# Moving the activations of the projections to another place in SBUF, by gaps between the pools

## The chip, the cores and the metric

The kernel runs on one core of a Trainium2 chip. The metric is the device time of one execution in microseconds. Three executions of the kernel before took 1711.0, 1717.55 and 1719.35 us, a median of 1717.55. A fourth one was taken by the hardware profiler: it took 1714.88 us, of which the profile's span covers 1713.1.

## The reference, cut to what matters

Three transformer blocks follow each other on one sequence of 256 tokens with 1024 features, all in float32:

```python
x = first_block(x, ...)    # forgetting attention, then sparse attention with compressed keys
x = second_block(x, ...)   # stick-breaking and dilated attention, then a gated feed-forward layer
return third_block(x, ...) # pooling and attention branches, then peer_ffn

def peer_ffn(h, w_q, sub_keys, u_tab, v_tab):
    q = (hf @ w_q).reshape(T, PEER_HEADS, 2, PEER_HALF)
    ...                    # two top-16 lists per head, their 16 best sums, softmax: e_c, g_c
    a = gelu(einsum('cd,chkd->chk', x_c, u_tab[e_c]))
    return einsum('chk,chkd->cd', g_c * a, v_tab[e_c])
```

The kernel does not gather the experts of `peer_ffn`: it multiplies the tokens with all 16,384 rows of `u_tab` and of `v_tab` and weights the experts that were not chosen with zero. So nearly all of its work is matrix products of 256 tokens with float32 weights that are read once from HBM.

## The kernel before, in words

**Weights.** The weights come in a fixed list of blocks of 128x1024 float32 (512 KB). `Weights.split` (lines 228 to 245) loads a block into `wraw` and splits it: ScalarE rounds it to fp32r, a format of TensorE with fewer bits, into `whi` (line 241), and VectorE writes the rest to `wlo` (line 242). Each split block has a number, counted from 0. `whi` and `wlo` lie in the pool `part`, which has three places for each; a block whose number leaves 3 when divided by 4 lies in the pool `extra` instead, as long as the number is under `until`, which comes to 232 (line 238). Block numbers 248 to 375 are those of `u_tab`, 376 to 503 those of `v_tab`.

**Products.** An activation is split in the same way into `hxh` and `hxl`, each 128 partitions x 8 x 256. A product of two split numbers is three matmuls, with the weights as the stationary operand (128x128) and the activation as the moving one (256 columns): `mm3`, lines 448 to 452. A weight block in `proj` is 8 times `mm3`, 24 matmuls. In the feed-forward layer `down` (lines 1204 to 1206) does the same with `fah` and `fal` as the moving operand. In `proj_nat` (lines 496 to 498) and in the last stage (line 1624) the roles are swapped: the activation is stationary and the weights move, 512 columns at a time.

**Stages in order of time.** Up to some 870 us the program has the five layers ahead of `peer_ffn`: projections whose results feed an attention that is woven between the matmuls, or the feed-forward layer (about 510 to 695 us). From some 874 us follow the queries of `peer_ffn` (16 blocks); then `proj(128, hx, ...)` (line 1601) multiplies with `u_tab`, and between its matmuls, every 42 of them or so, stand 12 matmuls of 128 columns (line 1584) that spread the gate weights over the experts. From 1355 us on, line 1624 multiplies with `v_tab`.

**Where tiles lie.** Pools lie behind each other in SBUF in the order in which they are opened; a tile's address is the same in all 128 partitions. Two pools hold split activations: `hxp` (line 279, the outer one, with inputs of projections) and `hxe` (line 1693, outputs of attention that enter the out-projections and the tile `mg`). `wp` (line 1605), the activations of the last stage, takes the place of `hxl` in `hxp`. The tiles of a layer (`ph`, with `fah` and `fal` among them) are allotted behind `extra`. The order of the program's instructions on an engine is the order in which the Python code issues them.

Of the kernel before, what the change touches and what calls it, by code (L numbers as in the profile page):

```python
# [9 lines left out]
F32 = mybir.dt.float32  # L10
F32R = mybir.dt.float32r
# [7 lines left out]
P = 128  # L19
D = 1024  # L20
S = 256
# [184 lines left out]
class Weights:  # L206
# [40 lines left out]
    def next(self):  # L247
        self.split(self.nu + 1 + self.ahead)
        self.nu += 1
        return self.p.pop(self.nu - 1)  # L250
# [20 lines left out]
def program(tc, A, out, upto=99):  # L271
    nc = tc.nc
    ctx = ExitStack()
    with ctx:
        cst = ctx.enter_context(tc.tile_pool(name="cst", bufs=1))
        big = ctx.enter_context(tc.tile_pool(name="big", bufs=1))
        raw = ctx.enter_context(tc.tile_pool(name="raw", bufs=4))
        part = ctx.enter_context(tc.tile_pool(name="part", bufs=3))
        hxp = ctx.enter_context(tc.tile_pool(name="hxp", bufs=1))
        ps = ctx.enter_context(tc.tile_pool(name="ps", bufs=2, space=PSUM))  # L280

# [1095 lines left out]
        def peer(hx, ph, hp):  # L1377
# [224 lines left out]

            tc.keep_in_program_order(nc.scalar.preload_act_table_set("natural_log_exp_and_others"))
            xN, gf = token_major()
            wp = hxp.tile([P, 3, 2, S], F32R, name="hxl")
            acc = [[ps.tile([P, 512], F32, name=n) for _ in range(2)] for n in ("s", "t")]
            chunks = {}

# [30 lines left out]
        def token_major():  # L1639

            xN = hxp.tile([P, 2, D], F32, name="hxh")
            for tb in range(2):
                for h in range(2):
                    p = ps.tile([P, 512], F32, name="o")
                    for k in range(4):
                        nc.tensor.transpose(p[:, k * P:k * P + P], xT[:, 4 * h + k, tb * P:tb * P + P], ident)
                    nc.scalar.copy(xN[:, tb, h * 512:h * 512 + 512], p)
            gf = [xT[:, 4 * i:4 * i + 4, :].rearrange("p a b -> p (a b)") for i in range(2)]
            for h in range(2):
                p = ps.tile([P, 512], F32, name="pj")  # L1650
                for k in range(4):
                    nc.tensor.matmul(p[:, k * P:k * P + P], mod(5)[:, 4 * h + k:4 * h + k + 1].to_broadcast([P, P]), ident,
                                     start=True, stop=True)
                nc.scalar.copy(gf[0][:, h * 512:h * 512 + 512], p)
            nc.sync.dma_start(gf[1], A["fin3"].to_broadcast([P, D]))
            return xN, gf
# [33 lines left out]
        with ExitStack() as early:  # L1690
            cp = early.enter_context(tc.tile_pool(name="cp", bufs=1))
            wk = early.enter_context(tc.tile_pool(name="wk", bufs=3))
            hxe = early.enter_context(tc.tile_pool(name="hxe", bufs=1))
            W.extra = early.enter_context(tc.tile_pool(name="extra", bufs=1))
            con = cp.tile([P, A["consts"].shape[1]], F32, name="con")
            nc.sync.dma_start(con, A["consts"])
            off = 0
            for n, m in CONSTS.items():
                C[n] = con[:, off:off + m]
                off += m  # L1700
            st = Rms(V["g0"])
            for kt in range(8):
                st.parts(kt)
                if kt == 0:
                    W.split(1)
            for i, blk in enumerate((fox, nsa, mixer2, ffn2, mixer3)):
                if i >= upto:
                    break
                i_blk = i
                if i == 2:  # L1710
                    cbp = tc.alloc_tile_pool(name="cbp", bufs=1)
                with tc.tile_pool(name=f"ph{i}", bufs=1, reuse_waits="tile") as ph:
                    st = blk(st)
                if i == 3:
                    cbp.release()
        if upto > 5:
            with tc.tile_pool(name="ph5", bufs=1, reuse_waits="tile") as ph, tc.tile_pool(name="hp", bufs=1, reuse_waits="tile") as hp:
                st = peer(st, ph, hp)
            with tc.tile_pool(name="ph6", bufs=3, reuse_waits="tile") as ph:
                wk = ph  # L1720
                finish_peer(*st)
        else:
            nc.sync.dma_start(out, xT)
# [5 lines left out]
def build(ins, upto=99):  # L1729
    import concourse.bacc as bacc  # L1730
    nc = bacc.Bacc("TRN2", target_bir_lowering=False, num_devices=1)
    A = {k: nc.dram_tensor("in_" + k, v.shape, mybir.dt.from_np(v.dtype), kind="ExternalInput").ap()
         for k, v in ins.items()}
    out = nc.dram_tensor("out_0_dram", (P, 2, D) if upto > 5 else (P, 8, S), F32, kind="ExternalOutput").ap()
    with tile.TileContext(nc) as tc:
        program(tc, A, out, upto)
    return nc
# [9 lines left out]
```

## Time and profile before

| | |
|---|---|
| median of three executions | 1717.55 us |
| profiled execution, its span | 1714.88 us, 1713.1 us |
| TensorE (PE) matmuls busy | 1658.1 us, 97% of the span |
| VectorE (DVE) busy | 1304.1 us, 76% |
| ScalarE (ACT) busy | 976.3 us, 57% |
| mean load of DMA | 175 GB/s |

How to read the rows below. A row of part 5 of the page or of a list of waits says what it holds in words: line, engine, operation, tiles; then the busy time of all, the mean of one, and the idle time just ahead of them with its cause. A row of the timeline gives a start in us, a length in us, and the instruction; x12 means twelve of them merged in one row. Matmuls are pipelined: the next one starts while the one before is still under way, so the pace of TensorE is the distance between two starts, not the length. A row of the table of stretches gives the stretch, its length, the busy time of PE, PEld (weight loads), DVE, ACT and POOL with the number of instructions, the granted clock of TensorE (1.00 is full), the share of DMA and its GB/s.

### The profile page before, as it was taken

What the parts mean: (1) busy time and instruction counts of PE and PEld (TensorE: products, weight loads), DVE (VectorE), ACT (ScalarE), POOL (GpSimd) and SP (SyncE); (2) the same over time, 40 slices, a digit from 0 to 9 for tenths busy, and PEclk for the clock granted to TensorE, in tenths of its full rate; (3) what the DMA queues carried; (4) which work ended last, traced back from release to release, by engine and by line L of the source; (5) the groups of instructions that cost most, each with busy time, mean ns of one, the idle gap of its engine ahead of it and who ended that gap; (6) DMA issues with size and microseconds to landing.
All of it is one profiled execution on the core that took longest, in us unless ns stands there. A gap on an engine that the chain in (4) does not pass through costs nothing.

```text
span 1713.1 us, 31723 instructions
## 1 busy us (share of the span) xinstructions
PE 1658.1 (97%) x12052; PEld 1532.3 (89%) x12052; DVE 1304.1 (76%) x2715; ACT 976.3 (57%) x1853; POOL 189.4 (11%) x198
## 2 busy tenths in 40 slices
PE   9999999989899999999999999999999999999997
PEld 7999888778789999889999999999999988888886
DVE  6887878699867766786768988888999566666665
ACT  5775567558855555566544455554444555555554
POOL 2000244340130000111046000000000000000000
PEclk9999999999999999999999999999999999999999
DMA  7444542387437877435555555454454556555663
GB/s 252 136 136 150 169 166 64 105 268 243 149 111 259 267 262 245 143 118 173 175 172 161 161 164 157 159 161 156 155 161 159 174 195 196 190 193 195 196 189 120
DMA packets 84088, 300.07 MB, mean 175 GB/s; under 512 B 10144, under 2 KB 11040, under 8 KB 83680
## 3 DMA queue, kind: packets, MB, share of 16 engines
q1 hardware_dynamic: 83360, 296.39, 53.5%
q8 instruction: 94, 1.54, 0.4%
q10 hardware_dynamic: 576, 1.66, 0.3%
q14 instruction: 58, 0.48, 0.1%
HBM read 296.04 MB, written 1.05 MB: 173 GB/s over the span
## 4 chain that ended last, share of the span: by engine, by line
PE 52%; DVE 3%; ACT 0%; issue 0%; POOLq 0%; POOL 0%; DVEq 0%; ACTq 0%
PE s L1624 10%; PE t L1624 10%; PE pj L450 5%; PE pj L451 5%; PE pj L452 5%; PE o L1584 3%; PE s L450 2%; PE t L450 2%; PE s L452 2%; PE s L451 2%; PE t L451 2%; PE t L452 2%; DVE wlo L242 1%; PE s L1433 0%; PE o L595 0%
## 5 line engine op out<-in xcount | busy, mean ns | idle before, releaser
L241 ACT CAST whi<-wraw 128x1024 fp32r<-128x1024 f32 x504 | 528.9, 1051 | 359.0 <-PE pj L451 108.7
L242 DVE TENSOR_TENSOR wlo<-wraw,whi 128x1024 fp32r<-128x1024 f32 x486 | 601.1, 1241 | 168.2 <-ACT whi L241 165.7
L450 PE MATMUL pj<-hxh,whi 128*128 128x256 f32 x1448 | 417.0, 288 | 7.0 <-DVE vl L602 4.5
L452 PE MATMUL pj<-hxh,wlo 128*128 128x256 f32 x1448 | 410.5, 284 | 1.2 <-DVE wlo L242 0.9
L451 PE MATMUL pj<-hxl,whi 128*128 128x256 f32 x1448 | 410.8, 284 | 0.6 <-DVE hxl L1193 0.3
L450 PEld LDWEIGHTS pj<-hxh,whi 128*128 128x128 f32 x1448 | 276.4, 191 | 11.6 <-DVE vl L602 5.4
L451 PEld LDWEIGHTS pj<-hxl,whi 128*128 128x128 f32 x1448 | 276.2, 191 | 2.7 <-DVE hxl L1193 1.0
L452 PEld LDWEIGHTS pj<-hxh,wlo 128*128 128x128 f32 x1448 | 276.0, 191 | 2.9 <-DVE wlo L242 1.7
L1624 PE MATMUL s<-whi,hxl 128*128 128x512 f32 x512 | 157.8, 389 | 0.0
L1624 PE MATMUL t<-whi,hxl 128*128 128x512 f32 x512 | 157.6, 389 | 0.0
L1612 ACT CAST hxl<-a 128x256 fp32r<-128x256 f32 x128 | 52.1, 408 | 152.0 <-PE t L1624 150.2
L450 PE MATMUL s<-hxh,whi 128*128 128x256 f32 x456 | 130.7, 287 | 1.7 <-DVE st L572 1.7
L452 PE MATMUL s<-hxh,wlo 128*128 128x256 f32 x456 | 129.0, 283 | 0.4 <-DVE wlo L242 0.4
L451 PE MATMUL s<-hxl,whi 128*128 128x256 f32 x456 | 128.9, 283 | 0.0
L450 PE MATMUL t<-hxh,whi 128*128 128x256 f32 x432 | 124.6, 288 | 1.3 <-ACT whi L241 1.3
L452 PE MATMUL t<-hxh,wlo 128*128 128x256 f32 x432 | 122.8, 284 | 1.7 <-DVE wlo L242 1.5
L451 PE MATMUL t<-hxl,whi 128*128 128x256 f32 x432 | 122.4, 283 | 0.0
L1624 PEld LDWEIGHTS t<-whi,hxl 128*128 128x128 f32 x512 | 96.1, 188 | 19.9
L1624 PEld LDWEIGHTS s<-whi,hxl 128*128 128x128 f32 x512 | 95.9, 188 | 20.0 <-ACT hxl L1612 0.2
L1613 DVE TENSOR_TENSOR hxl<-a,hxl 128x256 fp32r<-128x256 f32 x128 | 54.3, 425 | 62.6 <-PE t L1624 60.5
L291 DVE SCALAR_TENSOR_TENSOR wraw<-wraw,cb 128x1024 f32<-128x1024 f32 x48 | 59.6, 1241 | 44.5 <-DMA wraw<-in_ada 44.2
L450 PEld LDWEIGHTS s<-hxh,whi 128*128 128x128 f32 x456 | 87.0, 191 | 2.1 <-issue 1.9
(409 smaller groups left out, 3401.5 us busy)
## 6 DMA issues: line engine op xcount, KB each, us to landing
wraw<-in_pu SPq DMA_DIRECT2D x128, 512.0 KB
wraw<-in_pv SPq DMA_DIRECT2D x128, 512.0 KB
wraw<-in_b_ffn SPq DMA_DIRECT2D x66, 512.0 KB
wraw<-in_ada SPq DMA_DIRECT2D x48, 512.0 KB
wraw<-in_b_qk SPq DMA_DIRECT2D x24, 512.0 KB
wraw<-in_fox_qk SPq DMA_DIRECT2D x16, 512.0 KB
wraw<-in_b_o SPq DMA_DIRECT2D x16, 512.0 KB
wraw<-in_b_g SPq DMA_DIRECT2D x16, 512.0 KB
```

What stands on the lines that cost most here:

```text
L241: nc.scalar.copy(hi, r)
L242: (nc.gpsimd if self.np in self.on_pool else nc.vector).tensor_tensor(lo, r, hi.bitcast(F32), op=OP.subtract)
L291: nc.vector.scalar_tensor_tensor(t, t, 1.0, cb, op0=OP.mult, op1=OP.mult, accum_out=modT[:, i:i + 1])
L450: nc.tensor.matmul(o, wh, xh, start=start, stop=False)
L451: nc.tensor.matmul(o, wh, xl, start=False, stop=False)
L452: nc.tensor.matmul(o, wl, xh, start=False, stop=stop)
L1584: nc.tensor.matmul(p[:, t, :], x[:, w[0], :, w[1]], y[i][:, w[0], :, w[1]], start=i == 0 and t == 0, stop=i == 2, skip_group_check=True)
L1612: nc.scalar.copy(ah, src)
L1613: nc.vector.tensor_tensor(al, src, ah.bitcast(F32), op=OP.subtract)
L1624: nc.tensor.matmul(acc[tb][h], x[:, t], w[:, h * 512:h * 512 + 512], start=n == 0 and i == 0, stop=n == P - 1 and i == 2)
```

## The change

The change adds five unused tiles ("gaps") between pools and shifts `wp` inside its tile by 16 elements (64 bytes). No instruction is added, removed or moved on any engine, and the waits of all instructions are the same; what differs is the SBUF addresses.

```diff
         part = ctx.enter_context(tc.tile_pool(name="part", bufs=3))
+        gaps = iter(range(9))
+
+        def gap(ctx, n):
+            ctx.enter_context(tc.tile_pool(name=f"gap{next(gaps)}", bufs=1)).tile([P, n // 4], F32, name="gap")
+
+        gap(ctx, 192)
         hxp = ctx.enter_context(tc.tile_pool(name="hxp", bufs=1))
...
-            wp = hxp.tile([P, 3, 2, S], F32R, name="hxl")
+            wp = hxp.tile([P, 16 + 6 * S], F32R, name="hxl")[:, 16:].rearrange("p (n i s) -> p n i s", n=3, i=2)
...
             wk = early.enter_context(tc.tile_pool(name="wk", bufs=3))
+            gap(early, 192)
             hxe = early.enter_context(tc.tile_pool(name="hxe", bufs=1))
+            gap(early, 64)
             W.extra = early.enter_context(tc.tile_pool(name="extra", bufs=1))
+            gap(early, 192)
```

The addresses that the pools give in the two programs, in bytes within a partition, and what is left of them modulo 256:

| tiles | before | after |
|---|---|---|
| `whi`, `wlo` in `part` | 43,296 and steps of 4,096: 32 | the same: 32 |
| `whi`, `wlo` in `extra` | 132,960 and 137,056: 96 | 133,408 and 137,504: 32 |
| `hxh`, `hxl` in `hxp` | 67,872 and 76,064: 32 | 68,064 and 76,256: 224 |
| `hxh`, `hxl` in `hxe` | 116,576 and 124,768: 96 | 116,960 and 125,152: 224 |
| `fah`, `fal` of the feed-forward layer | 152,416 and on, steps of 1,024: 96 | 153,056 and on: 224 |
| `wp` | 76,064 and steps of 1,024: 32 | 76,320 and on: 32 |

The parts of a tile that one matmul reads start at multiples of 512 or 1,024 bytes in it, so they have the same remainder. The distance from the weights to the activation, modulo 256, of the program's matmuls:

| matmuls | activation and weights in | before | after |
|---|---|---|---|
| 6,168 of `mm3` | `hxp` with `part` or `hxe` with `extra` (32 less 32, 96 less 96) | 0 | 192 |
| 720 of `mm3` | `hxe` or a layer's tiles with `part` | 64 | 192 |
| 840 of `mm3` | `hxp` with `extra` | 192 | 192 |
| 408 and 120 of `down` | `fah`, `fal` with `part` and with `extra` | 64 and 0 | 192 |
| 1,536 of line 1624 | `wp` with `part` | 0 | 0 |

The 288 matmuls of `proj_nat`, in which the weights move, have the distance from activation to weights at 0 (216 of them) or 64 (72, block in `extra`) before, and all at 64 after.

## Rows read from the trace of the kernel before

**Rows 1.** The page: busy time by engine, and two groups of matmuls.

```profile
PE 1658.1 (97%) x12052; PEld 1532.3 (89%) x12052; DVE 1304.1 (76%) x2715; ACT 976.3 (57%) x1853; POOL 189.4 (11%) x198
...
L450 PE MATMUL pj<-hxh,whi 128*128 128x256 f32 x1448 | 417.0, 288 | 7.0 <-DVE vl L602 4.5
...
L1624 PE MATMUL s<-whi,hxl 128*128 128x512 f32 x512 | 157.8, 389 | 0.0
```

**Rows 2.** What PE waited for, longest first: the first two.

```profile
PE pj L450 <- DVE vl L602: 4.5, 2, 3.4
PE t L616 <- POOL pn L578: 3.2, 3, 1.4
```

**Rows 3.** Stretches: attention, feed-forward, routing, `u_tab` early and late.

```profile
300.00:420.00 120.00, 110.89 (x745) 95.84 (x744) 100.10 (x212) 75.83 (x162) 35.74 (x42) 0.99 0.62 207
520.00:700.00 180.00, 176.56 (x1464) 174.89 (x1463) 127.39 (x185) 94.99 (x143) 0.00 (x0) 1.00 0.77 253
960.00:1000.00 40.00, 36.95 (x301) 35.16 (x300) 39.71 (x72) 19.77 (x32) 0.00 (x0) 1.00 0.56 173
1000.00:1040.00 40.00, 40.00 (x382) 39.70 (x380) 31.17 (x70) 21.58 (x50) 0.00 (x0) 1.00 0.48 158
1200.00:1320.00 120.00, 120.00 (x1131) 119.05 (x1130) 114.11 (x231) 56.02 (x131) 0.00 (x0) 1.00 0.49 159
```

**Rows 4.** Timeline of PE in the `u_tab` stage, one round.

```profile
1005.59 0.86 PE L1584 MATMUL o<-ohy,ohx 128*128 128x128 bf16 x12
1006.26 0.36 PE L450 MATMUL t<-hxh,whi 128*128 128x256 f32 x1
1006.46 0.28 PE L451 MATMUL t<-hxl,whi 128*128 128x256 f32 x1
...
1007.40 0.28 PE L450 MATMUL pj<-hxh,whi 128*128 128x256 f32 x1
...
1010.64 0.86 PE L1584 MATMUL o<-ohy,ohx 128*128 128x128 bf16 x12
```

**Rows 5.** Timeline of PE, feed-forward layer: blocks 135 and 136.

```profile
553.31 0.28 PE L450 MATMUL pj<-hxh,whi 128*128 128x256 f32 x1
...
556.04 0.28 PE L450 MATMUL pj<-hxh,whi 128*128 128x256 f32 x1
...
558.92 0.28 PE L1204 MATMUL s<-fah,whi 128*128 128x256 f32 x1
```

**Rows 6.** Timeline of PE, feed-forward layer: block 127, behind block 126.

```profile
530.46 0.28 PE L450 MATMUL o<-hxh,whi 128*128 128x256 f32 x1
...
533.28 0.28 PE L1204 MATMUL s<-fah,whi 128*128 128x256 f32 x1
```

**Rows 7.** Timeline of PE, third block: two stretches of three blocks in `part`.

```profile
825.02 0.28 PE L450 MATMUL pj<-pph,whi 128*128 128x256 f32 x1
...
833.50 0.28 PE L450 MATMUL pj<-pph,whi 128*128 128x256 f32 x1
...
858.45 0.28 PE L450 MATMUL pj<-hxh,whi 128*128 128x256 f32 x1
...
866.61 0.28 PE L450 MATMUL t<-hxh,whi 128*128 128x256 f32 x1
```

**Rows 8.** Timeline of PE, first attention: block 15 behind three transposes.

```profile
58.84 0.49 PE L616 MATMUL t<-ident,pn 128*128 128x128 f32 x3
59.08 0.37 PE L450 MATMUL pj<-hxh,whi 128*128 128x256 f32 x1
...
59.52 0.28 PE L450 MATMUL pj<-hxh,whi 128*128 128x256 f32 x1
...
60.55 0.39 PE L628 MATMUL o<-pth,vh 128*128 128x512 f32 x1
```

**Rows 9.** Timeline of PE, `proj_nat`: end of block 2, all of block 3.

```profile
18.10 0.39 PE L496 MATMUL s<-whi,hxh 128*128 128x512 f32 x1
...
18.78 0.40 PE L496 MATMUL s<-whi,hxh 128*128 128x512 f32 x1
...
21.54 0.40 PE L496 MATMUL s<-whi,hxh 128*128 128x512 f32 x1
```

## The prediction

> **What bounds the kernel now.** I read the page first: PE is busy for 1658.1 of 1713.1 us, and its largest groups are the 256-column matmuls of `mm3` and the 512-column ones of line 1624 [rows 1]. Then the list of what PE waited for: the longest entry is 4.5 us in total, the next 3.2 [rows 2]. So PE waits for almost nobody by name; it is bound by its own pace. The table of stretches says where another engine is close: in the `u_tab` stage PE is busy for 40.00 of 40 us while DVE has 31.17, but DVE reaches 39.71 of 40 in the routing stretch and 114.11 of 120 late in the stage [rows 3]. In the attention stretches PE itself has holes (110.89 of 120). The granted clock is 1.00 or 0.99 in all of them, the 2.4 GHz level, so the clock is no part of the argument. Last I read the timeline for the distance between starts, since that is what PE's pace is.
>
> **What the pace depends on in the trace.** The kernel before already contains every distance between activation and weights of the table, except the ones beyond 256 bytes, so the trace can be asked.
>
> At distance 0 (the `u_tab` stage), 27 matmuls (nine times `mm3`) lie between 1007.40 and 1010.64 us: 3.24 us / 27 = 120.0 ns each [rows 4]. Block 136, in `part`, does the same in another layer: 558.92 - 556.04 = 2.88 us / 24 = 120.0 ns [rows 5].
>
> At distance 192 (block 135, in `extra`, right ahead of it, same activation): 556.04 - 553.31 = 2.73 us / 24 = 113.8 ns [rows 5]. But block 127, also at 192, takes 533.28 - 530.46 = 2.82 us / 24 = 117.5 ns [rows 6].
>
> At distance 64 there are the same two paces, and each holds over a long stretch: 72 matmuls in 8.48 us, 117.8 ns, and 72 in 8.16 us, 113.3 ns [rows 7].
>
> So I read it thus: at 0 the pace is 120.0 ns and nothing else; at 64 and 192 it is one of two, 113.3 (quick) or 117.8 (slow), and a stretch keeps what it began with until something breaks the run. What chooses? Block 127 is slow and comes directly behind a block at distance 0, without a break; block 135 is quick and starts behind other matmuls. Block 15, also at 192, starts afresh behind three transposes, and is at (60.55 - 59.52) / 9 = 114 ns after a few matmuls [rows 8]. After the change no block at distance 0 is left to inherit from, and in the `u_tab` stage every round starts afresh: the first matmul behind the 12 of line 1584 lasts 0.20 us to the next start (1006.26 to 1006.46), as the one behind the transposes does (59.08 to 59.29) [rows 4, 8]. I take the quick pace there. Elsewhere I take the middle, 115.6 ns, since both occur.
>
> One rule speaks against all this. The Trainium skill, page SBUF — State Buffer, section "Who interferes with whom", says that PE has two independent read ports, one for the moving operand and one for weight loads, and that "PE and ACT never wait on anyone". By that rule addresses don't matter and the time would stay at 1714.9 us. Rows 5 show two blocks of the same instructions, the same activation and no wait, 2.73 and 2.88 us long, so the trace disagrees.
>
> **The change part by part**, against the profiled execution's 1714.9 us:
>
> 1. `u_tab` stage and queries: (16 + 128) blocks x 24 = 3,456 matmuls go from distance 0 to 192. at the quick pace, 113.6 ns as the mean of 113.8 and 113.3, 120.0 - 113.6 = 6.4 ns each: -22.1 us. Part of it is not to be had, since DVE's work doesn't shrink. From 960 to 1000 us DVE is idle for 0.3 us, so nearly all of that stretch's saving is lost (some 250 of the 301 matmuls are of 256 columns, 250 x 6.4 ns = 1.6 us; +1.3). From 1200 to 1320 us it is idle for 5.9 us, and PE would save about 840 x 6.4 ns = 5.4 us: PE would ask for nearly all of DVE's idle time, of which I expect two thirds to be usable (+2). What is late then is the one-hot products that line 1584 reads. Net -18.8.
> 2. The other 6,168 - 3,456 = 2,712 matmuls at 0, ahead of 870 us: 120.0 - 115.6 = 4.4 ns, -11.9 us. In the attention stretches PE is in a hole for some 8% of the time, and a faster PE meets its softmax partners earlier and waits for them; I take off a quarter: -9.
> 3. The 720 of `mm3` and 408 of `down` at 64 go to 192: two paces before, two after, 0. If all were quick before and slow after, 1,128 x 4.5 ns = +5; the reverse -5. The 120 of `down` at 0: -0.5.
> 4. `proj_nat`: 216 matmuls of 512 columns go from 0 to 64. At 0 three take 18.78 - 18.10 = 0.68 us, 227 ns each; at 64 the twelve of block 3 take 2.76 us, 230 ns [rows 9]. 216 x 3 = +0.65.
> 5. Line 1624: `wp` is shifted so that its remainder stays 32; 1,536 matmuls at an unchanged distance, 0.
> 6. All other tiles move as well. Reads and writes of DVE, ACT and DMA at other remainders: no row shows an effect apart from PE's, and the tiles of a layer keep their distance to each other. I take 0. From both sides: the 31.17 us of DVE in 40 leave it room for 20% in most of the `u_tab` stage; a DVE slower by 2% in the two full stretches would cost 0.02 x 160 = 3 us, one faster by 2% would give as much.
> 7. DMA has to bring the weights sooner: 159 GB/s in 1200 to 1320 us become 159 x 120.0 / 113.6 = 168, against 253 that it moves in the feed-forward layer [rows 3]. Hidden.
>
> Sum: -18.8 - 9 - 0.5 + 0.65 = -27.6, so 1687.3 us against 1714.9. The median of the three runs is 2.7 us over the profiled one; with the same difference the runs after have a median near 1690.
>
> **The rivals.**
>
> - *The slow pace holds nearly everywhere.* The start of a round behind line 1584 may choose it; for it speaks that the stretch from 825 us kept it over 72 matmuls. Against it: blocks 15 and 135. 3,456 x 2.3 = 7.9 and 2,712 x 2.3 = 6.2 with a quarter off, 4.7; the stretches that are quick now at 64 lose up to half of 1,128 x 4.5 = 2.5; with `proj_nat` 9.5 us are left: 1708 by the runs' median. A mixture of both paces in the `u_tab` stage lies between, near 1699.
> - *Nothing changes* (within 0.5%, which is about what a measurement of this kernel can tell from no change). The distance may stand for something else in rows 5, such as what ran before the block; or the time PE saves comes back as waits for DVE in routing and attention. Against it: outside of 960 to 1000 and 1200 to 1320 us the `u_tab` stage has DVE free for a fifth of the time. 1717. The rule of the Trainium skill cited above would give this too.
> - *Slower, by the last stage.* The remainder is kept modulo 256 only. Modulo 512 the distance of `wp` from the weights goes from 0 to 256, and that of `hxp` from `part` becomes 192 where blocks 15 and 135 have 448. Should a step of 512 be what counts, the projections may keep their 120.0 ns, and the 1,536 matmuls of line 1624 go from 227 to the 230 of block 3, +4.6 us: 1717.5 + 4.6 + 0.65 = 1723; at 236 ns each it would be 1732. Against a gain of 27 us it decides from 1,536 x 18 ns on. For it speaks only that no row shows those two distances.
>
> **How the numbers follow.** Quick pace in the `u_tab` stage: 0.57, 1690 us, by itself from 1679 (all of 6,168 x 6.4 = 39 us) to 1699. Slow pace or a mixture: 0.28, 1699 to 1708. No change: 0.10. Slower: 0.05. The range has to reach over the slow pace above; below, all quick with DVE's part lost is 1717.5 - 39.5 + 3.3 - 0.65, some 1681, and the two 5 us of point 3 go to 1677. So 1677 to 1708. 0.5% of 1717.5 is 8.6 us, that is 1709 and 1726. Faster: 0.57 + 0.25 = 0.82; same: 0.03 of the slow pace, 0.10 and 0.01 make 0.14; slower 0.04.
>
> **What the profile after would show.** Step 1: rounds of the `u_tab` stage with starts 113 to 114 ns apart behind the first few; at 117 to 118 the first rival holds, at 120 the second. The stage from 874 to 1355 us would last about 19 us less. DVE close to 40 of 40 from 1200 us on, and new waits of PE for `ohx` or `ohy` of some us. Step 2: the layers ahead of 870 us shorter by about 9 us, most in the feed-forward layer, where PE has no holes. Step 4: `proj_nat` at 230 ns. Step 5: line 1624 still at 227 ns and its stage unchanged; if it isn't, the third rival is at work. I am wrong if starts at distance 192 are 120 ns apart, or if they are 113 and the span has not followed.

## The result and the profile after

The changed kernel takes 1696.15 us (median of 4 runs, 1694.25 to 1699.57), the kernel before beside it 1716.61 (4 runs, 1711.0 to 1719.35): a ratio of 0.9884, 95% interval 0.9867 to 0.9901. That is 20.5 us less; the forecast was 27.6 less, 1690 us, in a range of 1677 to 1708. The profiled execution took 1694.25 us with a span of 1692.4, against 1714.9 and 1713.1, so that the two profiles differ by 20.7 us and their stages may be compared one by one. `mm3` is now at lines 458 to 460, `down` at 1212 to 1214, the one-hot products at 1592, the last stage at 1632.

The page after, the rows that answer to [rows 1]:

```profile
PE 1628.3 (96%) x12052; PEld 1500.7 (89%) x12052; DVE 1301.9 (77%) x2715; ACT 976.2 (58%) x1853; POOL 189.4 (11%) x198
...
L458 PE MATMUL pj<-hxh,whi 128*128 128x256 f32 x1448 | 411.9, 285 | 7.7 <-DVE vl L610 5.2
...
L1632 PE MATMUL s<-whi,hxl 128*128 128x512 f32 x512 | 157.7, 389 | 0.0
```

The change moves no instruction: the counts are those of before, and the mean length of one matmul hardly differs (285 ns against 288). Matmuls overlap, so that column can't show the pace; only the distance from start to start can. In the timeline of PE, one round of the `u_tab` stage (columns as in [rows 4]):

```profile
999.94 0.86 PE L1592 MATMUL o<-ohy,ohx 128*128 128x128 bf16 x12
1000.61 0.36 PE L458 MATMUL t<-hxh,whi 128*128 128x256 f32 x1
1000.81 0.28 PE L459 MATMUL t<-hxl,whi 128*128 128x256 f32 x1
...
1001.38 0.28 PE L458 MATMUL pj<-hxh,whi 128*128 128x256 f32 x1
...
1004.44 0.28 PE L458 MATMUL pj<-hxh,whi 128*128 128x256 f32 x1
1004.79 0.86 PE L1592 MATMUL o<-ohy,ohx 128*128 128x128 bf16 x12
```

From 1001.38 to 1004.44 lie 27 starts: 3.06 us / 27 = 113.3 ns, where [rows 4] have 120.0. The first start behind the one-hot products still takes 0.20 us.

The stretches of [rows 3] in the profile after (the later ones moved to where the same work now is):

```profile
300.00:420.00 120.00, 110.26 (x732) 95.84 (x732) 98.22 (x212) 76.75 (x165) 32.32 (x39) 0.97 0.61 203
520.00:700.00 180.00, 174.19 (x1466) 170.94 (x1466) 128.92 (x193) 96.45 (x148) 0.00 (x0) 1.00 0.77 255
955.00:995.00 40.00, 35.87 (x306) 34.12 (x304) 39.73 (x68) 19.57 (x32) 0.00 (x0) 1.00 0.52 171
995.00:1035.00 40.00, 40.00 (x394) 39.75 (x392) 32.50 (x74) 22.88 (x55) 0.00 (x0) 1.00 0.50 164
1183.00:1303.00 120.00, 120.00 (x1187) 119.15 (x1186) 117.36 (x238) 59.02 (x138) 0.00 (x0) 1.00 0.50 163
```

Three things are to be seen. In the `u_tab` stage PE is still full (120.00 of 120), and DVE has risen to 117.36 without becoming the bound: 1,187 matmuls where 1,131 stood. In routing DVE was full and is full (39.73 of 40). And in the feed-forward layer (520 to 700) PE, which had 3.4 us of idle time, now has 5.8, beside an unchanged DMA share of 0.77.

PE's longest waits, where [rows 2] had 4.5 and 3.2 us:

```profile
PE pj L458 <- DVE vl L610: 5.2, 2, 4.0
PE s L1213 <- DVE fal L1226: 4.2, 6, 0.9
PE t L841 <- ACT g L516: 3.9, 1, 3.9
```

All three stand in the layers ahead of 871 us, and all three were there before, shorter (4.5, 3.0 and 2.8 us): a PE that is quicker comes earlier to partners that are not.

Since both programs have the same matmuls in the same order, the time from each start to the next can be subtracted, matmul by matmul, and added up by stage. What each kernel saves (minus: shorter) against the kernel before, or, in the last two columns, against its own counterpart below; times are those of before:

| stage, us | after | after, again | `hxp` only | 112 | no `w_ada`, feed-forward | no `w_ada` |
|---|---|---|---|---|---|---|
| 0 to 163 | -2.1 | -1.9 | -1.1 | -1.3 | -1.6 | -1.3 |
| 163 to 205 | +0.6 | -1.8 | -0.1 | +0.5 | -0.1 | -2.1 |
| 205 to 346 | -1.8 | -3.5 | -1.6 | -0.2 | -0.4 | -0.4 |
| 346 to 470, second mixer | +2.0 | +2.9 | +0.9 | +1.0 | +0.3 | -0.9 |
| 470 to 517 | +0.2 | -0.2 | +0.1 | -0.6 | -0.1 | -0.5 |
| 517 to 697, feed-forward | -2.0 | -0.8 | -0.9 | -2.0 | -7.7 | -7.8 |
| 697 to 871, third block | -0.4 | -0.5 | -1.7 | -3.0 | -0.6 | -0.6 |
| 871 to 931, queries | -1.8 | -1.9 | -1.8 | -1.8 | -1.8 | -1.8 |
| 931 to 993, routing | 0.0 | 0.0 | +0.7 | +0.1 | 0.0 | 0.0 |
| 993 to 1351, `u_tab` | -15.4 | -15.4 | -14.5 | -13.3 | -15.4 | -15.3 |
| 1351 to the end | 0.0 | 0.0 | 0.0 | +0.1 | 0.0 | 0.0 |
| sum | -20.6 | -23.1 | -20.0 | -20.5 | -27.3 | -30.6 |

From 871 us on, the changed kernel's two profiles and the two pairs without `w_ada` agree within 0.2 us (17.1 to 17.3 less); `hxp` alone has 15.6 less and 112 has 15.0. The rest of the spread and the missing time are ahead of 871 us: 3.5 us in the first profile of the changed kernel, 5.8 in the second.

How much of that is pace can be told by adding up only the starts that follow closely on each other in both profiles. Ahead of 871 us the matmuls came 12.3 us closer together, and 8.8 us came back elsewhere: 3.5 in the feed-forward layer, 2.9 in the second mixer, 1.8 from 163 to 205 us, 0.6 in the other four together.

### The profile page after: what moved, and what is told of

It reads as the page before. It is cut to its first block, busy times and chain, and to the rows that moved or that the text cites. A ratio compares the mean times of both kernels' runs of the same rounds, so it can differ in the third digit from the quotient of the medians.

```text
span 1692.4 us, 31723 instructions
## 1 busy us (share of the span) xinstructions
PE 1628.3 (96%) x12052; PEld 1500.7 (89%) x12052; DVE 1301.9 (77%) x2715; ACT 976.2 (58%) x1853; POOL 189.4 (11%) x198
## 5 line engine op out<-in xcount | busy, mean ns | idle before, releaser
L458 PE MATMUL pj<-hxh,whi 128*128 128x256 f32 x1448 | 411.9, 285 | 7.7 <-DVE vl L610 5.2
L460 PE MATMUL pj<-hxh,wlo 128*128 128x256 f32 x1448 | 405.1, 280 | 1.7 <-DVE wlo L242 1.1
L459 PE MATMUL pj<-hxl,whi 128*128 128x256 f32 x1448 | 405.5, 280 | 0.7 <-DVE hxl L1201 0.4
```

The source lines that it names most:

```text
L458: nc.tensor.matmul(o, wh, xh, start=start, stop=False)
L459: nc.tensor.matmul(o, wh, xl, start=False, stop=False)
L460: nc.tensor.matmul(o, wl, xh, start=False, stop=stop)
```

## The experiments

**The pace by the distance alone.** A kernel of nothing but such matmuls, which computes none of the layers: `whi`, `wlo` at fixed addresses, the activation read at an offset that is moved by 16 bytes from stretch to stretch, 48 matmuls each.

```diff
+        for d in range(0, 512, 16):
+            run(0, 1)      # 24 matmuls at distance 0; in other sets transposes, or 12 bf16 ones
+            run(d)         # 48 at distance d
```

> This kernel leaves all of the blocks out and holds only matmuls on one pair of weights and one pair of activations, with the moving activation read from 0, 16, 32, ... 496 bytes past the weights modulo 512; each stretch has 48 matmuls of 256 columns. Set 1 starts each stretch behind three transposes, set 2 behind twelve bf16 matmuls of 128 columns, set 3 directly behind 24 matmuls at distance 0; set 4 has the activation stationary and the weights moving, 512 columns. Theory (the distance modulo 256 sets the pace): 120.0 ns between starts at 0 and 256; at 64 and 192 113.3 or 117.8 ns, 192 quick in sets 1 and 2 and slow in set 3; 448 as 192, 320 as 64. Rival (a step of 512 counts): 256 is not 120 ns and 192 is not as 448. Rival (the distance doesn't matter, but what ran before): all distances of a set at one pace. Set 4: 227 ns at 0, about 230 at 64.

One thing ran otherwise than expected: in set 1 the transposes of the first 14 distances (0 to 208) ran ahead of all stretches, so that those stretches stand directly behind each other. At distances 112 and 192 (and 368, 448) the last 24 starts of a stretch were 113.33 ns apart, in all three sets; at 0 and 256, 120.00; at all others 116.7 to 120.0, among them 64 with 117.8. 256 more bytes change the settled pace by 1.5 ns at most, and it differs by up to 2.2 ns between the sets at one distance. The 113.3 ns that 72 matmuls at 64 had in the kernel before [rows 7] did not come here, so what settles in this kernel is not all that a distance can do. In the timeline, behind 24 matmuls at distance 0, the stretch at 192 (start, its 25th matmul, the next stretch):

```profile
521.18 0.29 PE L56 MATMUL o<-xhi,whi 128*128 128x256 f32 x1
...
523.92 0.28 PE L56 MATMUL o<-xhi,whi 128*128 128x256 f32 x1
...
526.64 0.28 PE L56 MATMUL o<-xhi,whi 128*128 128x256 f32 x1
```

and the one at 64:

```profile
452.76 0.28 PE L56 MATMUL o<-xhi,whi 128*128 128x256 f32 x1
...
455.59 0.28 PE L56 MATMUL o<-xhi,whi 128*128 128x256 f32 x1
...
458.42 0.29 PE L56 MATMUL o<-xhi,whi 128*128 128x256 f32 x1
```

523.92 to 526.64 is 24 x 113.3 ns, 455.59 to 458.42 is 24 x 117.9. A stretch at 192 does not keep the pace of the block at 0 that it follows; here it lost it within a few matmuls. So the reading of block 127 [rows 6] as slow by inheritance is not borne out here.

**A distance of 256.** The kernel before with all of `hxp` and what follows 256 bytes further:

```diff
+        ctx.enter_context(tc.tile_pool(name="gap", bufs=1)).tile([P, 64], F32, name="gap")
```

> The kernel before with one gap of 256 bytes ahead of hxp: every tile behind it moves, and every distance modulo 256 stays. Theory: the pace stays at 120.0 ns in the u_tab stage, and the time within 0.3% of the kernel before (1717). Rival (moving the tiles is what helps, or a step of 512 counts): up to the 20 us of the change, near 1697; or another pace than 120.0.

1716.13 us against 1715.43, ratio 0.9999 (0.9987 to 1.0011). In the timeline of its `u_tab` stage 27 starts still take 3.24 us, 120.0 ns:

```profile
1005.05 0.28 PE L451 MATMUL t<-hxh,whi 128*128 128x256 f32 x1
...
1008.29 0.28 PE L451 MATMUL t<-hxh,whi 128*128 128x256 f32 x1
```

So it is not that the tiles move at all; with the scan above, what counts is the remainder modulo 256.

**One part alone.** Only `hxp` moves, and what follows is put back on its old remainder:

```diff
+        gap(ctx, 192)                 # ahead of hxp; wp shifted as in the change
+            gap(early, 64)            # ahead of hxe; none ahead of extra or the layers' tiles
```

> Only the tiles of `hxp` are moved by 192 bytes (a gap of 192 ahead of the pool, one of 64 ahead of `hxe` that puts all that follows back on its old remainder); `wp` keeps its remainder of 32. So distance 192 for `hxp` with `part` (all of the `u_tab` stage, the queries and most early projections), while `hxe` with `extra` stays at 0, `hxe` and the layers' tiles with `part` at 64, and `hxp` with `extra` comes to 128. Theory: the time from 871 us on depends on `hxp` with `part` alone, so that part is shorter by the same 17 us (pace 113.5 ns in the `u_tab` stage), and the layers ahead of it are where they were within 2 us, since what they gain in pace they give back in waits: 1697 to 1701. Rival: the 3.5 us that the whole change kept ahead of 871 us come from the blocks in `extra` and from `down`; then that part is unchanged or, with `hxp` with `extra` at 128 (118 ns in the scan of distances), 2 us longer: 1700 to 1703, with the feed-forward layer 2 us longer than in the changed kernel. Rival: the remainders of the other tiles matter for the `u_tab` stage; then it keeps over 115 ns.

1695.52 us (ratio 0.9901, 0.9885 to 0.9918): as short as with the whole change, and below the 1697 to 1701 that I expected. Its `u_tab` stage has the quick pace, 27 starts in 3.05 us:

```profile
1002.09 0.28 PE L458 MATMUL pj<-hxh,whi 128*128 128x256 f32 x1
...
1005.14 0.28 PE L458 MATMUL pj<-hxh,whi 128*128 128x256 f32 x1
```

The first rival, that the blocks in `extra` and `down` bring what is kept ahead of 871 us, falls: 4.4 us are kept there without them, and 3.5 with them. The feed-forward layer is 1.1 us longer than in the changed kernel, but the third block 1.3 us shorter: its stretches of three blocks, at 192 up to 818 us and at 64 from 832 us on, ran at the quick pace, where the changed kernel has 117.8 ns. The second falls by the pace. (The 0.7 us more in routing are 3.4 us at the 1.2 GHz level, from 986 us on, of the profiles in the table in this one alone. The `u_tab` stage saved 0.9 us less, most of it not as pace: its mean is 113.5 ns in both.)

**Weight transfers in the feed-forward layer.** 26 of the 92 blocks that come in during that layer are `w_ada` blocks, which VectorE consumes and PE never sees. Both kernels without them (what they would have given is left out):

```diff
-ADA = {"b2_v": range(2, 8), "b2_qk": range(16), "b2_ffn": {*range(7, 64, 3), *range(8, 50, 6)}}
+ADA = {"b2_v": range(2, 8), "b2_qk": range(16), "b2_ffn": ()}
```

> The kernel before without the 26 blocks of w_ada that are loaded during the feed-forward layer (their 26 values are left at 1). It serves as the base for after_noada. If weight transfers hold up the feed-forward layer already in the kernel before, its stretch (some 180 us) gets shorter by a few us; the distances are as before, 120.0 and 117.8 ns.

> The same without these 26 blocks in the changed kernel. Theory (the quicker PE of the feed-forward layer ran into the weight transfers, which gave back 3.5 of 5.5 us): against before_noada the feed-forward layer is now shorter by 4 to 5.5 us, where the change itself made it shorter by 2.0. Rival (it waits for the chain of ScalarE and VectorE behind the gate, not for transfers): again only about 2 us.

1709.1 and 1681.74 us, one run each: the new distances are now worth 27.4 us, and the layer is 7.7 us shorter instead of 2.0. The stretch from 510 to 690 us, columns as in [rows 3], in the kernel before, the changed one, and these two:

```profile
510.00:690.00 180.00, 176.53 (x1473) 174.99 (x1472) 126.69 (x181) 96.24 (x148) 0.00 (x0) 1.00 0.77 255
```
```profile
510.00:690.00 180.00, 174.26 (x1490) 171.84 (x1489) 127.69 (x184) 97.98 (x151) 0.00 (x0) 1.00 0.78 258
```
```profile
510.00:690.00 180.00, 180.00 (x1517) 179.83 (x1516) 103.25 (x133) 98.16 (x152) 0.00 (x0) 1.00 0.57 187
```
```profile
510.00:690.00 180.00, 179.89 (x1547) 178.33 (x1547) 109.82 (x147) 101.87 (x162) 0.00 (x0) 1.00 0.59 196
```

With the `w_ada` blocks, 255 and 258 GB/s: the weights come hardly faster after than before, and PE waits. Without them PE is full, and 187 become 196. ScalarE, which splits the weights, waits longer for them, first before, then after (engine, line, what it waited for: us in total, times, longest):

```profile
ACT whi L241 <- DMA wraw<-in_b_ffn: 27.8, 25, 4.5
```
```profile
ACT whi L241 <- DMA wraw<-in_b_ffn: 37.0, 35, 4.5
```

That is not to say that the DMA engines are the limit: their share is 0.77 and not 1. VectorE makes a pass of 1.2 us over each `w_ada` block, and only then is its place in `wraw` free for the next transfer. The changed kernel, what VectorE waited for and what the queue that starts the transfers (SP) waited for from 510 to 690 us, and two stretches of 2 us:

```profile
DVE wraw L299 <- DMA wraw<-in_ada: 44.3, 24, 3.3
SPq L224 <- DVE wraw L299: 57.6, 19, 4.5
566.00:568.00 2.00, 2.00 (x20) 2.00 (x19) 0.19 (x1) 1.48 (x3) 0.00 (x0) 1.00 0.98 387
568.00:570.00 2.00, 2.00 (x20) 2.00 (x19) 2.00 (x3) 1.29 (x3) 0.00 (x0) 1.00 0.15 55
```

The two take turns: for 2 us the transfers run at 387 GB/s while VectorE stands before a `w_ada` block that has not landed, then VectorE works off what stood behind it while 55 GB/s are moved. So 258 GB/s is not what the transfers can do at most. Leaving out the blocks takes away their transfers, their passes on VectorE and their places in `wraw` together: that the `w_ada` blocks held the layer is shown, which of the three did it is not.

The matmuls of the layer ran 5.5 us quicker in the changed kernel, and 3.5 us came back as waits of PE. The other 2.2 us of the 7.7 are pace: without the waits all starts of `mm3` from 520 to 680 us are at 113 to 114 ns, and with them 55 to 100% by stretches of 40 us (in the second profile from under 10 to 100%). A wait ends a run, and what comes behind it may go on slow (below).

**Moving some of them ahead.**

```diff
-"b2_ffn": {*range(7, 64, 3), *range(8, 50, 6)}
+"b2_o": range(8), "b2_ffn": {*range(7, 61, 3)}
```

> The changed kernel with 8 of the 26 `w_ada` blocks of the feed-forward layer moved ahead, one behind each block of the second layer's output projection. Theory: the feed-forward layer of the changed kernel waits for weight transfers; with 8 of 92 blocks less it ends about 2 us sooner, and the output projection, in which the queue has room, loses less than 0.5 us: 1693 to 1695. Rival: the transfers are only moved, the output projection waits for them by the same amount: 1696 to 1697.

1697.33 us (ratio 0.9909, 0.9889 to 0.9929), where 1693 to 1695 were expected: nothing is won. The layer was 1.0 us shorter than in the changed kernel, but the output projection and its surroundings (470 to 517 us) took 2.0 us more, all of it as waits. So the rival holds in its sum, but not in its cause: the waits that are new there are not those for weights but for VectorE, itself or by way of GpSimd, at the norm behind the projection, on an engine that now has eight `w_ada` passes more there.

```profile
PE o L428 <- POOL acc L423: 1.3, 1, 1.3
PE o L429 <- DVE xT L642: 0.7, 1, 0.7
```

(346 to 470 us took 2.2 us more; in that profile it has 10.2 us at the 1.2 GHz level, against 3.4, so that says nothing of the transfers.)

**All of them away.** The same two without any `w_ada` block (`ADA = {}`).

> The kernel before without any of the 48 `w_ada` blocks (their results are left out: the modulation is a constant), so that its 22 blocks of the second mixer (346 to 470 us) are gone too. It is the measure for the next kernel; some 1700, since 26 blocks less took 6 us.

> The changed kernel, likewise without the 48 `w_ada` blocks. In four profiles the second mixer (346 to 470 us) came out 0.9 to 2.9 us longer with the new distances, though its matmuls ran quicker. Theory (there too it is the queue of weight transfers, with DVE's pass over each `w_ada` block in it, that takes the saving back): against the kernel before without these blocks the stage is 0.5 to 1.5 us shorter. Rival (the waits are those on the softmax chain, DVE and POOL, which do not depend on the transfers): still 0.5 to 2 us longer. By the first the whole difference to the kernel before without these blocks is 28 to 30 us, by the second 26 to 28.

1699.72 and 1669.09 us, one run each: 30.6 less. Some 2 us of that are not the distances' doing: the stretch from 163 to 205 us has 3.4 us at the 1.2 GHz level in the first of the two profiles and none in the second. The second mixer is 0.9 us shorter instead of 2.0 longer. Of its waits, the one that [rows 2] and the profile after have at the top is down to 0.9 us in both (it was 3.4 us in this stage before, 4.0 after and 4.9 in the second profile of after); first without the change, then with it:

```profile
PE pj L451 <- DVE vl L603: 0.9, 1, 0.9
```
```profile
PE pj L459 <- DVE vl L611: 0.9, 1, 0.9
```

So here too the `w_ada` blocks go with what took the saving back. The granted clock fell to the 1.2 GHz level for 3.4 us at 378.2 us in the changed kernel's profile, just as PE ended this wait (374.2 to 378.3), and at 374.9 us in its second one, again at the end of the wait (370.2 to 375.1); the 15 starts in such a piece took 1.5 and 1.4 us more than the same ones before. In the profile of before the clock stayed up behind a wait of 3.4 us, and in the two without `w_ada` there is neither the wait nor the piece. Every profile of the changed distances with `w_ada` blocks in this stage has such a piece at or behind the wait, and so have those of the old distances with 256 bytes more and without the feed-forward layer's `w_ada` (waits of 4.3 and 4.5 us). So the piece goes with this wait and not with the distances, and what the wait alone costs isn't shown. The stretch from 163 to 205 us shows what such a piece does; PEclk is the third number from the end; before, after, and the changed kernel profiled again:

```profile
163.00:205.00 42.00, 38.63 (x265) 35.52 (x264) 32.55 (x41) 22.57 (x26) 7.86 (x3) 0.96 0.50 155
```
```profile
163.00:205.00 42.00, 37.55 (x261) 34.34 (x260) 32.57 (x42) 22.11 (x24) 7.83 (x3) 0.92 0.50 153
```
```profile
163.00:205.00 42.00, 38.60 (x283) 35.90 (x282) 34.66 (x43) 22.86 (x25) 7.84 (x3) 1.00 0.52 169
```

The same kernel lost 0.6 us in that stage at a clock of 0.92, and won 1.8 at 1.00. Up to the last 7 us the half clock took 13.65 us of the profile of before and 13.65 of that of after, so it explains single stages, and not the difference of the two.

**The other quick distance.** `hxp` at 112 in place of 192 (the rest as in the changed kernel):

```diff
-        gap(ctx, 192)
+        gap(ctx, 96)
+                return [pool.tile([P, 8 * S + m], F32R, name=n)[:, 4:4 + 8 * S].rearrange(...) ...]
```

> The changed kernel with the tiles of `hxp` at remainder 144, distance 112 to `part` and to `extra`, in place of 192 (`wp` stays at 32, `hxe` and the layers' tiles at 224). In the scan of distances 112 was the only other one that ran at 113.3 ns. Theory (the pace comes from the distance alone and both are the same): the `u_tab` stage at 113.5 ns, the layers ahead of it with the same mixture of 113.3 and 117.8 ns, 1694 to 1699. Rival (at 192 the quick pace is lost easily, and 112 holds it better): the blocks from 790 to 843 us at 113.3 instead of 117.8 ns, 2 us less there and up to 3 us less in all, 1691 to 1694. Rival (the scan does not carry over): pace of 117 or 120 ns in the `u_tab` stage, 1705 or more.

1694.95 us (ratio 0.9895, 0.9878 to 0.9911): the first theory, in sum. In parts it was off: the third block is 2.6 us shorter than in the changed kernel (it has the quick pace from 800 us on, as the first rival had it), and the `u_tab` stage 2.1 us longer, at a mean of 114.3 ns in place of 113.5.

**What holds the slow pace.** From 792 to 866 us all blocks of the changed kernel run at 117.8 ns, at distance 192. Small matmuls ahead of ten of these blocks:

```diff
+                    for r in BREAK.get(len(blocks) if i_blk == 4 else -1, ()):
+                        nc.tensor.matmul(p[:, j, 0:r], w[0][:, 0:P], x[0][:, 0, 0:r], start=True, stop=True)
```

> The changed kernel with small extra matmuls ahead of ten blocks of the third block's gate and output projections (one, two or three of 128 columns, one of 64, one of 256; what they write is overwritten by the block's first matmul). In the changed kernel all blocks from 792 to 868 us run at 117.8 ns, though their distance is 192. Theory (a stretch keeps the pace it began with until something breaks the run): behind the breaks the pace is drawn anew, and some blocks run at 113.3 ns up to the next break; with half of 24 blocks quick, 24 x 24 x 4.5 / 2 = 1.3 us less there, less some 2 us that the extra matmuls take. Rival (something lasting in this stretch sets the pace, such as what the other engines read and write there): 117.8 ns behind every break. Either way 1695 to 1699 in all.

1695.69 us, one run. The timeline of PE around one break of 128 columns (797.37) and one of 64 (802.95):

```profile
797.37 0.22 PE L482 MATMUL pj<-hxh,whi 128*128 128x128 f32 x1
...
799.89 0.28 PE L462 MATMUL pj<-hxh,whi 128*128 128x256 f32 x1
...
802.61 0.28 PE L462 MATMUL pj<-hxh,whi 128*128 128x256 f32 x1
802.95 0.19 PE L482 MATMUL pj<-hxh,whi 128*128 128x64 f32 x1
...
803.41 0.28 PE L462 MATMUL pj<-hxh,whi 128*128 128x256 f32 x1
...
808.36 0.28 PE L462 MATMUL pj<-hxh,whi 128*128 128x256 f32 x1
```

799.89 to 802.61: 24 starts in 2.72 us, 113.3 ns. 803.41 to 808.36: 42 in 4.95, 117.9. The pace holds over two blocks on either side and changes at the breaks, so that a break can change the pace is shown, and the lasting influence falls: same distance, same neighbours on the other engines, two paces. Behind 64 columns it was slow both times, behind one of 128 columns quick twice and slow once, behind two or three of them quick; one of 256, which is a matmul like the others, changed nothing.

**Two breaks as an improvement**, and the changed kernel once more beside it.

```diff
+BREAK = {18: (128, 128), 28: (128, 128)}
```

> The changed kernel with two extra matmuls of 128 columns ahead of two blocks of the third block's projections: the first gate block behind the pooling matmuls, and the first block of the output projection. In the kernel with ten breaks every stretch behind two or three such matmuls went on at 113.3 ns, and both behind one of 64 columns at 117.8. Theory (the start sets the pace of the whole stretch): 240 + 192 matmuls from the pooling to the output projection, and some 186 of the output projection, at 113.3 instead of 117.8 ns, 618 x 4.5 = 2.8 us less, some 0.5 us for the two restarts: 2.3 us less than the changed kernel beside it. Rival (chance decides behind each start): one or both stretches stay at 117.8 ns, 0 to 1.5 us less. Rival: PE's time comes back as waits in the third block: the pace is 113.3, but the stage from 790 to 871 us is not shorter.

> The changed kernel as it is, as the measure for the kernel with the two restarts: 1694 to 1697, 790 to 871 us at 117.8 ns as in its first profile if the program's order sets the pace; should the pace there differ from one execution to the next, the stretch is at 113.3 ns now.

1693.28 us (ratio 0.9872, 0.9853 to 0.9892) against 1696.32 (0.9889, 0.9873 to 0.9906): the intervals overlap, so a gain isn't shown. Half of the theory failed: the first of the two stretches, 432 matmuls, stayed at 117.8 ns behind the same two extra matmuls, the second went to 113.3. In the second profile of the changed kernel the stretch from 792 us was slow again, while the feed-forward layer had under a tenth of its starts at the quick pace from 520 to 560 us where the first profile had all. What at a start decides between the two paces stays open; it is not the number of columns alone.

## Why the prediction was right, and where it was off

In sum 7.0 us too much was forecast, 1.6 of them in step 1 and 5.4 in step 2.

- *The mechanism* was right: distance 0 to 192 turns 120.0 into 113.3 ns where nothing else limits PE, and a distance of 256 does nothing. What chooses between the two paces was not: inheritance from a block at 0 is not borne out. The rule of the Trainium skill that the prediction weighed, page SBUF — State Buffer, section "Who interferes with whom", that PE's two read ports are independent and PE waits on no one, would give no change; the runs with nothing but PE at work (120.00 and 113.33 ns) disagree with it.
- *Step 1, queries and `u_tab`*: -18.8 forecast, -17.2 measured. The quick pace was right, over 97% of the starts of the `u_tab` stage, but 22.1 us was too much for it: the matmuls came 19.6 us closer together, since the mean over the stage went from 119.6 to 113.5 ns and the starts around the one-hot products did not change. DVE's two parts were mis-sized in opposite ways, so that it is luck that their sum, 2.5, is near the 3.3 of the forecast: in routing it took back the whole gain, 2.5 us of 2.5 (forecast 1.3, from a stretch of 40 us where the stage has 62); late in the `u_tab` stage, at 117.36 of 120 us, it took back nothing, and not 2. The waits for `ohx` and `ohy` that I expected did not come.
- *Step 2, the 2,712 matmuls ahead of 870 us* is the mis-sized term. Forecast: 11.9 at a middle pace, a quarter off for waits in attention, -9, with -0.5 for `down` and +0.65 for `proj_nat` 8.9 together. Measured: the matmuls did come 12.3 us closer, so the mixture of two paces was right in size; but 3.5 us of the time is left (5.8 in the second profile), not 8.9. What was wrong is the quarter: 8.8 us came back and not 3. I looked for the holes in attention, and took the feed-forward layer, where PE had 176.56 of 180 us [rows 3], as the place without any. The row's 253 GB/s I read as room for the `u_tab` stage in step 7, and not as a sign that this layer hangs on its transfers. Without the `w_ada` blocks the layer gains 7.7 us instead of 2.0; 3.5 of these 5.7 are waits that the blocks brought, 2.2 are pace that went with them. The second mixer is the other place, 2.9 us, and 1.8 us from 163 to 205 us are in part the clock.
- *Step 3*: 0 forecast. From 790 to 871 us, where blocks at 64 and at 0 went to 192, 0.2 us more were measured: those at 64 that had been quick (from 858 us on in [rows 7]) became slow, those at 0 went from 120.0 to 117.8 ns; the bound of 5 us was never near.
- *Step 4*: 216 x 3 ns = +0.65 forecast, some +0.3 measured. Block 4 of `proj_nat`, at 64, takes 2.75 us for twelve, 229 ns, against 227 at distance 0 [rows 9]:

```profile
20.48 0.39 PE L504 MATMUL s<-whi,hxh 128*128 128x512 f32 x1
...
23.23 0.59 PE L704 MATMUL o<-acc,ones 128*128 128x256 f32 x2
```

- *Steps 5 and 6*: line 1632 is unchanged (0.02 us over the stage), and nothing was lost or won by other tiles at new remainders that the runs could tell.
- *Step 7, DMA hidden*: right for the `u_tab` stage (163 GB/s); in the feed-forward layer the way by which the weights come was not hidden, as above.
- *The rivals.* The slow pace nearly everywhere did not come about, though it exists at 192: behind the one-hot products the quick one came. A step of 512 plays no role that these runs could tell (120.0 ns with 256 bytes more, 1.5 ns at most in the scan).
- *The range*: its lower end subtracts the 0.65 us of `proj_nat`, which should have been added, so 1682 and not 1681; nothing hangs on it.

## What to carry to other kernels

When PE is full and its matmuls are small, measure from start to start, by the remainder of the difference of the two operands' addresses, before touching the schedule: the same instruction sequence had 113.3 and 120.0 ns in it. Ask of every stage what is second to PE there, the transfers included: a stage in which PE is busy for 98% may be held by the chain that brings its weights, and then gives a faster PE little. If that chain is the limit, take other work off it in that stage; moving it next door only moved the waits.

## What was not expected of the hardware

- Of 16 distances modulo 256 only 112 and 192 settle at 113.33 ns in the kernel of matmuls alone; the others at 116.7 to 120.0. In the full kernel 64 has the quick pace too, over 72 matmuls [rows 7]. With 512 moving columns and the weights moving, 0 settles at 226.7 ns (mean of the last twelve), the others at 228 to 234.
- At 192 a second steady pace of 117.8 ns exists in the full kernel, lasts over some 600 matmuls, and can end when smaller matmuls come between; in the kernel of matmuls alone no stretch settled at it at this distance.
- PE's weight loads in the stretches at distance 0 are recorded at 192 ns, and at 187 and 188 ns in those at 192, but also in those at 64, whose pace is 117.8 ns there.
